# A decoder layer on one core: MLP weight sums by accumulating DMA with reordered products, and half of the last gate in seven products

## The chip, the core and the metric

The kernel runs on one core of a Trainium2 chip. Its engines each work through their own instruction list in order and meet by semaphores: PE (TensorE, matmuls), DVE (VectorE, elementwise), ACT (ScalarE, activations and copies), POOL (GpSimd, here an issuer of DMAs) and SP (SyncE, the issuer of the other DMAs). The metric is device time in microseconds of one execution; the median of three runs stands for a kernel.

## The reference, cut to what matters

One layer, 256 rows (`SEQ`) of 2048 columns (`D_MODEL`), all float32, `D_FF` = 8192:

```python
x = x + merged @ w_out[i]                       # two attention mixers, gated: not touched here
hm = rmsnorm(x, g_mlp[i])
x = x + jnp.square(jax.nn.relu(hm @ w_up[i])) @ w_down[i]
hp = rmsnorm(x, g_ple[i])
x = x + (p[i] @ w_ple_proj[i]) * jax.nn.sigmoid(hp @ w_ple_gate[i])
```

The change touches the product with `w_down` and the last line's product with `w_ple_gate` (2048 x 2048, "the gate").

## The kernel before

**Precision and splits.** Every weight comes as 1 MB of float32 in a `raw` tile (`load`, an SP DMA) and is split into a high part `wh` by ACT (L82) and a low part `wl` by DVE (L83), in two pieces of 128x1024; a tile pool gives `raw`, `wh` and `wl` three slots each, so a split can't begin before the slot of three pieces earlier has been read by PE. A product is three matmuls (high x high, high x low, low x high). Activations are split in the same way; where they are scaled, as at the turns, by L85 (ACT) and L86 (DVE).

**MLP.** The hidden dimension goes in eight groups s. `up_units(s)` computes hidden columns in 16 units of 8 pairs of matmuls (L525 of 512 columns, L526 of 256); `hidden` squares, and for the fast products forms four sums of the activations in `hr`, which has one buffer (L507 to L510), and splits them into a tile `u` of the pool `hid`. The down product of a group has two column halves. The second is plain (`plain_units`, 8 units of 12 matmuls, L627 to L629; results are added to the residual `xr` by `add_rows`, L454). The first (`fast_units`) uses a seven-product scheme on 2x2 blocks (as Strassen's): row blocks are the two 128-row tiles, the inner dimension and the columns are halved. Its seven products of 12 matmuls (L545, L547, L549) take four 1 MB quarters of the weight as they are, or sums of them: DVE adds one quarter to another in place (L559, four per group), `later(2, ...)`, two modelled microseconds after the product that still reads the old content. Partial results are copied from PSUM by ACT (`keep`, L555) and added to `xr` by DVE (L559 on `xr`, and L454).

**Order.** `together` interleaves the units of group s + 1's up product with group s's fast and plain units by fixed fractions; this makes seven periods between 713 and 1336 us. `advance` moves a modelled clock, and `later` emits work once that clock has come to its due time. What stands in an engine's list is fixed at build time.

**Gate.** After the last plain units (mixed with the embedding product, `embedding_units`) the residual is squared and summed (`squares_rows`) and turned: `turn` transposes with PE (L465, 8 per call) and splits. Four column groups of 96 matmuls follow (L724 to L726), two PSUM banks each, 16 loads of 1 MB. `gate_out` takes each result: ACT sigmoid (L712), DVE times the embedding (L713) and plus the residual (L714), DMA out.

Of the kernel before, what the change touches and what calls it, by code (L numbers as in the profile page):

```python
# [9 lines left out]
F32 = mybir.dt.float32  # L10
# [6 lines left out]
P = 128  # L17
# [42 lines left out]
def layer_kernel(ctx: ExitStack, tc: tile.TileContext, xt, xm, pt, gains, qkg, cst,  # L60
# [433 lines left out]
    FAST = [(s, 0) for s in range(7)]  # L494

    def hidden(s, fast):
# [40 lines left out]
    def fast_units(s, n, f):  # L537
# [46 lines left out]
        pz = bank("at")  # L584
        product(pz, S1, b[0, 0], True)
        z0 = keep(pz, 0)
        sum_later(b[0, 0], b[1, 1])
        yield
        sums()
        product(px, S2, b[0, 0], False)  # L590
        s2 = keep(px, 1)
        sum_later(b[0, 0], b[1, 0])
        yield
        sums()
        pw = bank("at")
        product(pw, A22, b[0, 0], True)
        w0 = keep(pw, 0)
        sum_later(b[0, 1], b[1, 1])
        yield
        py = bank("at")  # L600
        product(py, A12, b[1, 0], True)
        add(xr[1][:, left[0]], s1)
        add_rows(1, c1, py, r2[:, 1:2])
        yield
        sums()
        product(px, S3, b[0, 1], False)
        add(xr[0][:, left[0]], w0)
        add_rows(0, c1, px, r2[:, 0:1])
        add(xr[0][:, left[1]], z0)
        add_rows(0, c2, px, r2n)  # L610
        yield
        product(pz, S4, b[1, 1], False)
        nc.vector.tensor_tensor(xr[1][:, left[1]], xr[1][:, left[1]], s2, op=ALU.subtract)
        add_rows(1, c2, pz, r2[:, 1:2])
        yield

    def plain_units(s, n, u):

        for j in range(2):
# [15 lines left out]
            for tt in range(2):  # L635
                add_rows(tt, (2 * n + j) * PIECE, ps[tt], r2[:, tt:tt + 1])
# [16 lines left out]
    def embedding_units():  # L653
        em.extend(mw.tile([P, D], F32, tag="quart", name=f"em{tt}", bufs=4) for tt in range(2))
# [62 lines left out]
    for g in range(4):  # L717
# [10 lines left out]
        for tt in range(2):  # L728
            gate_out(g, tt, ps[tt], 0, PIECE)
# [64 lines left out]
```

## Time and profile before

| | us |
|---|---|
| median of three runs | 1487.3 (1486.57 to 1488.2) |
| the profiled execution | 1486.83 |
| its span | 1485.1 |
| PE busy | 1470.0 (99%) |
| DVE, ACT busy | 1002.1 (67%), 839.2 (57%) |
| seven MLP periods | 713 to 1336, 89.0 each |
| last MLP products and embedding | 1336 to 1390 |
| gate | 1390 to 1479, then results out until 1485.1 |

PE is the engine that sets the time. Matmuls overlap in it, so a start is a better mark than a busy time: from the start of one to the start of the next is what a matmul costs. In brackets behind an instruction of the timeline stands how long its engine was idle before it, and which instruction released it. The granted clock of PE is 1.00 at 2.4 GHz and 0.50 at 1.2 GHz.

### The profile page before, as it was taken

What the parts mean: (1) busy time and instruction counts of PE and PEld (TensorE: products, weight loads), DVE (VectorE), ACT (ScalarE), POOL (GpSimd) and SP (SyncE); (2) the same over time, 40 slices, a digit from 0 to 9 for tenths busy, and PEclk for the clock granted to TensorE, in tenths of its full rate; (3) what the DMA queues carried; (4) which work ended last, traced back from release to release, by engine and by line L of the source; (5) the groups of instructions that cost most, each with busy time, mean ns of one, the idle gap of its engine ahead of it and who ended that gap; (6) DMA issues with size and microseconds to landing.
All of it is one profiled execution on the core that took longest, in us unless ns stands there. A gap on an engine that the chain in (4) does not pass through costs nothing.

```text
span 1485.1 us, 17838 instructions
## 1 busy us (share of the span) xinstructions
PE 1470.0 (99%) x6960; PEld 1209.4 (81%) x6960; DVE 1002.1 (67%) x1209; ACT 839.2 (57%) x1084; POOL 49.2 (3%) x65
## 2 busy tenths in 40 slices
PE   8999999999999999999999999999999999999998
PEld 6788888888888888888787887878888788888886
DVE  5975555455555555556878879788787878766654
ACT  6545555488834444546655655656565655656543
POOL 0641000000000000000000000000000000000000
PEclk9999999999999999999999999999999999999999
DMA  8555544544455555557455564645546465444563
GB/s 334 197 193 179 172 167 169 174 167 171 171 197 197 173 197 184 185 193 289 142 201 195 175 225 141 227 168 197 200 157 238 144 205 194 154 144 167 206 218 109
DMA packets 40341, 279.09 MB, mean 188 GB/s; under 512 B 4624, under 2 KB 4880, under 8 KB 7104
## 3 DMA queue, kind: packets, MB, share of 16 engines
q1 hardware_dynamic: 39600, 275.01, 53.4%
q0 software_dynamic: 512, 2.92, 0.5%
q8 instruction: 54, 0.88, 0.2%
q14 instruction: 31, 0.25, 0.0%
q10 hardware_dynamic: 144, 0.02, 0.0%
HBM read 275.83 MB, written 2.10 MB: 187 GB/s over the span
## 4 chain that ended last, share of the span: by engine, by line
PE 91%; DVE 4%; issue 2%; ACT 1%; DMA 1%; SPq 0%; DVEq 0%; ACTq 0%
PE ps_mm L525 15%; PE ps_mm L139 13%; PE ps_mm L138 13%; PE ps_mm L137 13%; PE ps_mm L526 8%; PE ps_mm L628 4%; PE ps_mm L629 4%; PE ps_mm L627 3%; PE ps_at L547 3%; PE ps_at L545 2%; PE ps_at L549 2%; DVE wl L83 2%; ACT wh L82 1%; PE ps_at L725 1%; PE ps_at L724 1%
## 5 line engine op out<-in xcount | busy, mean ns | idle before, releaser
L83 DVE TENSOR_TENSOR wl<-raw,wh 128x1024 fp32r<-128x1024 f32 (+1 forms) x462 | 563.9, 1229 | 336.4 <-ACT wh L82 330.6
L82 ACT ACTIVATE wh<-raw 128x1024 fp32r<-128x1024 f32 (+1 forms) x462 | 484.9, 1053 | 388.6 <-PE ps_mm L139 209.4
L525 PE MATMUL ps_mm<-h,wh 128*128 128x512 f32 x1024 | 366.0, 398 | 0.0
L526 PE MATMUL ps_mm<-h,wl 128*128 128x256 f32 x1024 | 287.2, 281 | 0.4
L137 PE MATMUL ps_mm<-wh,h 128*128 128x512 f32 x640 | 254.9, 399 | 2.0 <-ACT wh L82 1.7
L138 PE MATMUL ps_mm<-wl,h 128*128 128x512 f32 x640 | 250.9, 392 | 1.2 <-DVE wl L83 1.1
L139 PE MATMUL ps_mm<-wh,h 128*128 128x512 f32 x640 | 250.8, 392 | 0.0
L525 PEld LDWEIGHTS ps_mm<-h,wh 128*128 128x128 f32 x1024 | 192.3, 188 | 46.2 <-ACT wh L82 2.2
L526 PEld LDWEIGHTS ps_mm<-h,wl 128*128 128x128 f32 x1024 | 193.2, 189 | 8.1 <-DVE wl L83 3.1
L83 DVE TENSOR_TENSOR wl<-quart,wh 128x1024 fp32r<-128x1024 f32 x98 | 120.0, 1224 | 83.7 <-ACT wh L82 83.5
L82 ACT ACTIVATE wh<-quart 128x1024 fp32r<-128x1024 f32 x98 | 104.0, 1061 | 123.4 <-PE ps_mm L525 89.1
L138 PEld LDWEIGHTS ps_mm<-wl,h 128*128 128x128 f32 x640 | 120.9, 189 | 27.9 <-DVE wl L83 3.9
L137 PEld LDWEIGHTS ps_mm<-wh,h 128*128 128x128 f32 x640 | 120.6, 189 | 28.1 <-ACT wh L82 4.4
L139 PEld LDWEIGHTS ps_mm<-wh,h 128*128 128x128 f32 x640 | 120.7, 189 | 25.5
L628 PE MATMUL ps_mm<-wl,u 128*128 128x512 f32 x256 | 101.9, 398 | 4.0 <-DVE wl L83 3.9
L629 PE MATMUL ps_mm<-wh,u 128*128 128x512 f32 x256 | 100.2, 391 | 0.0
L627 PE MATMUL ps_mm<-wh,u 128*128 128x512 f32 x256 | 98.0, 392 | 0.0
L547 PE MATMUL ps_at<-wl,u 128*128 128x512 f32 x196 | 80.4, 410 | 0.0
L545 PE MATMUL ps_at<-wh,u 128*128 128x512 f32 x196 | 78.6, 401 | 0.0
L549 PE MATMUL ps_at<-wh,u 128*128 128x512 f32 x196 | 76.8, 392 | 0.0
L559 DVE TENSOR_TENSOR quart<-quart 128x2048 f32<-128x2048 f32 x28 | 64.0, 2287 | 0.5
L628 PEld LDWEIGHTS ps_mm<-wl,u 128*128 128x128 f32 x256 | 48.1, 188 | 18.3 <-DVE wl L83 9.3
(198 smaller groups left out, 1704.8 us busy)
## 6 DMA issues: line engine op xcount, KB each, us to landing
raw<-in_wa SPq DMA_DIRECT2D x79, 1024.0 KB, 4.8
raw<-in_wup SPq DMA_DIRECT2D x64, 1024.0 KB, 4.8
raw<-in_wdn SPq DMA_DIRECT2D x36, 1024.0 KB, 4.8
quart<-in_wdn SPq DMA_DIRECT2D x28, 1024.0 KB, 4.8
raw<-in_wo SPq DMA_DIRECT2D x16, 1024.0 KB, 4.8
raw<-in_wpg SPq DMA_DIRECT2D x16, 1024.0 KB, 4.8
raw<-in_wba SPq DMA_DIRECT2D x8, 1024.0 KB, 4.8
raw<-in_wbb SPq DMA_DIRECT2D x8, 1024.0 KB, 4.7
```

Source lines behind the costliest of these rows:

```text
L82: nc.scalar.activation(hi, src, AF.Copy)
L83: nc.vector.tensor_tensor(lo, src, hi.bitcast(F32), op=ALU.subtract)
L137: nc.tensor.matmul(ps[tt], lhs[kt][:, 0, t], wh, start=kt == 0, stop=False)
L138: nc.tensor.matmul(ps[tt], lhs[kt][:, 0, t], wl, start=False, stop=False)
L139: nc.tensor.matmul(ps[tt], lhs[kt][:, 1, t], wh, start=False, stop=kt == last)
L525: nc.tensor.matmul(ps, wh, flat(h2[kt]), start=kt == 0, stop=False)
L526: nc.tensor.matmul(ps[:, :T], wl, h2[kt][:, 0, :], start=False, stop=kt == DT - 1)
L545: nc.tensor.matmul(ps, f[k][:, 0, a, :], wh, start=start and k == 0, stop=False, skip_group_check=not start)
L547: nc.tensor.matmul(ps, f[k][:, 0, a, :], wl, start=False, stop=False, skip_group_check=not start)
L627: nc.tensor.matmul(ps[tt], u[k][:, 0, a, :], wh, start=i + k == 0, stop=False)
L628: nc.tensor.matmul(ps[tt], u[k][:, 0, a, :], wl, start=False, stop=False)
L629: nc.tensor.matmul(ps[tt], u[k][:, 1, a, :], wh, start=False, stop=last)
```

## The change

**Weight sums in the MLP.** The four quarter tiles are gone. A tile `chain` (two buffers) is loaded with the first quarter; the running sums are made by DMAs that add in memory: `add_loaded` issues two of 512 KB from POOL after each product that read `chain`, three times per group. One other quarter is loaded into `right`, and DVE adds to it the quarter b11 (L569 of the changed kernel). b10 and b11 now come through the shared `raw` slots (14 loads there per period instead of 12; 19 MB per period from memory instead of 16). The seven products come in the order A11, A12, S1, S4, S2, S3, A22; partial results are not kept by ACT but added to `xr` at once from PSUM, by eight `add_rows` per group that are delayed by `later(0.6, ...)` or more into the next unit. The results of plain units are delayed in the same way.

**Gate.** Columns 0 to 1023 stay plain (`gate_plain`), columns 1024 to 2047 go by seven products over all rows (`gate_fast`), each of 24 matmuls (L792, L794, L795), mixed by `together`; 360 matmuls in all instead of 384. `turn_pair` turns two 128-column blocks at a time: four transposes (L686), two copies into `hr` (L690), four sums (L498 to L501), a split of 128x1024 on ACT and one on DVE. Two of the eight turned pairs (`h3u`) and the weights of the fast half (`gq`) live in the pool `hid`. Loads: 24 MB instead of 16 (`product` asks for its weight once per half, so A12's quarter is loaded twice), with 12 accumulating DMAs of 512 KB among them. `finish` adds a kept partial to the last one before `gate_out`.

```diff
-        px = bank("at")
-        product(px, A11, b[0, 0], True)
-        s1 = keep(px, 1)
-        sum_later(b[0, 0], b[0, 1])
-        yield
-        sums()
...
+        def add_loaded(q, i, j):
+            for k in range(0, 4, 2):
+                nc.gpsimd.dma_start(q[:, k:k + 2, :].rearrange("p k c -> p (k c)"),
+                                    wdn[s, n, i, j, :, k * PIECE:(k + 2) * PIECE],
+                                    accum_op=ALU.add)
...
+        chain = quarter("chain", 2, 0, 0)
         px = bank("at")
+        product(px, A11, chain, True)
+        add_loaded(chain, 0, 1)
+        later(0.6, add_rows, 1, c1, px, r2[:, 1:2])
+        yield
+        py = bank("at")
+        product(py, A12, load(wdn[s, n, 1, 0], 4, PIECE), True)
+        later(0.6, add_rows, 1, c1, py, r2[:, 1:2])
+        yield
+        pz = bank("at")
+        product(pz, S1, chain, True)
+        add_loaded(chain, 1, 1)
+        later(0.6, add_rows, 0, c2, pz, r2[:, 0:1])
+        right = quarter("right", 2, 0, 1)
+        yield
+        b11 = load(wdn[s, n, 1, 1], 4, PIECE)
+        product(pz, S4, b11, False)
+        later(0.6, add_rows, 1, c2, pz, r2[:, 1:2])
+        later(2, add, right, b11)
+        yield
+        product(px, S2, chain, False)
+        add_loaded(chain, 1, 0)
...
             for tt in range(2):
-                add_rows(tt, (2 * n + j) * PIECE, ps[tt], r2[:, tt:tt + 1])
+                args = tt, (2 * n + j) * PIECE, ps[tt], r2[:, tt:tt + 1]
+                if s < 7:
+                    later(0.6 + 1.5 * tt, add_rows, *args)
...
+    def turn_pair(k):
+        tp = bank("at")
+        for i in range(2):
+            for tt in range(2):
+                o = (2 * i + tt) * P
+                nc.tensor.transpose(tp[:, o:o + P],
+                                    xr[tt][:, (2 * k + i) * P:(2 * k + i + 1) * P], ident)
+        r = mw.tile([P, 8, P], F32, tag="hr", name="hr", bufs=1)
+        for i in range(2):
+            nc.scalar.activation(r[:, 2 * i:2 * i + 2, :].rearrange("p a t -> p (a t)"),
+                                 tp[:, i * T:(i + 1) * T], AF.Copy,
+                                 scale=gn[:, 2, 2 * k + i:2 * k + i + 1])
+        four_sums(r)
+        u = pair_tile(k)
+        split(u[:, 0], u[:, 1], r)
...
     def finished(g):
-        later(3, turn, g, h3, 2)
+        later(3, turn_pair, 2 * g)
+        later(4.5, turn_pair, 2 * g + 1)
...
+        chain = quarter(0, 0, room)
+        px, py = bank("at"), bank("at")
+        yield from product(px, A11, lambda c: chain[c], True, (0, 1))
+        keep_later("x", px)
+        yield
+        yield from product(py, A12, lambda c: load(wpg[1, 1, 0, c], 4, PIECE), True)
+        finish_later(0.6, 1, 0, "x", py, ALU.add)
...
+    together((0.9, 16, gate_plain()), (1.9, 14, gate_fast()))
```

**Three places in the order.** Names carry the number of their tile, `L` the line in the kernel that the row is of. First DVE in an MLP period of before, where an up unit's `hr` sums and low parts surround sums of quarters (L559):

```order
L507 TENSOR_TENSOR hr_8380<-hr_8380 128x128
L508 TENSOR_TENSOR hr_8380<-hr_8380 128x128
L83 TENSOR_TENSOR wl_8451<-quart_8431,wh_8450 128x1024
L509 TENSOR_TENSOR hr_8380<-hr_8380 128x128
L559 TENSOR_TENSOR quart_8431<-quart_8431,quart_8433 128x2048
L510 TENSOR_TENSOR hr_8380<-hr_8380 128x128
L83 TENSOR_TENSOR wl_8487<-raw_8484,wh_8486 128x1024
L83 TENSOR_TENSOR wl_8491<-raw_8484,wh_8490 128x1024
L83 TENSOR_TENSOR u_8386<-hr_8380,u_8386 128x1024
L532 TENSOR_TENSOR hs_8403<-ps_mm_8404,ev_8479 128x256
L559 TENSOR_TENSOR quart_8433<-quart_8433,quart_8435 128x2048
L83 TENSOR_TENSOR wl_8510<-raw_8507,wh_8509 128x1024
```

The like place of the changed kernel, DVE's list after the third and fourth fast product (`L535 hs` belongs to an up unit, `L454` are result adds, `chain` and `right` the new weight tiles):

```order
L83 TENSOR_TENSOR wl_7202<-raw_7199,wh_7201 128x1024
L454 SCALAR_TENSOR_TENSOR xr0_247<-ps_at_7154,r2_5039,xr0_247 128x512
L83 TENSOR_TENSOR wl_7206<-raw_7199,wh_7205 128x1024
L569 TENSOR_TENSOR right_7177<-right_7177,raw_7289 128x2048
L535 TENSOR_TENSOR hs_7126<-ps_mm_7127,ev_7196 128x256
L83 TENSOR_TENSOR wl_7225<-raw_7222,wh_7224 128x1024
L83 TENSOR_TENSOR wl_7229<-raw_7222,wh_7228 128x1024
L83 TENSOR_TENSOR wl_7292<-raw_7289,wh_7291 128x1024
L454 SCALAR_TENSOR_TENSOR xr0_247<-ps_mm_7010,r2_5039,xr0_247 128x512
L83 TENSOR_TENSOR wl_7303<-raw_7289,wh_7302 128x1024
L535 TENSOR_TENSOR hs_7126<-ps_mm_7221,ev_7264 128x256
L454 SCALAR_TENSOR_TENSOR xr1_248<-ps_mm_7011,r2_5039,xr1_248 128x512
L83 TENSOR_TENSOR wl_7318<-raw_7315,wh_7317 128x1024
```

The L559 sums of quarters between the low parts are gone but for one (L569); L454 result adds now stand there.

Second, ACT at the start of the gate before (`h3_2`, `h3_3` are turned columns, `wh` gate weights):

```order
L82 ACTIVATE wh_11084<-raw_11078 128x1024
L85 ACTIVATE h3_2_10766<-ps_at_11036,gn_75 128x256
L85 ACTIVATE h3_2_10766<-ps_at_11045,gn_75 128x256
L85 ACTIVATE h3_2_10766<-ps_at_11036,gn_75 128x256
L85 ACTIVATE h3_2_10766<-ps_at_11045,gn_75 128x256
L82 ACTIVATE wh_11125<-raw_11123 128x1024
L85 ACTIVATE h3_3_10767<-ps_at_11054,gn_75 128x256
L85 ACTIVATE h3_3_10767<-ps_at_11063,gn_75 128x256
L85 ACTIVATE h3_3_10767<-ps_at_11054,gn_75 128x256
```

and of the changed kernel (`h3u` are the last two turned pairs, `wh_11093` the high part of the fast half's first weight):

```order
L232 ACTIVATE junk_11019,ss2_5047<-xr1_248 128x512
L214 ACTIVATE rs_11102<-rv_11100 128x2
L690 ACTIVATE hr_11056<-ps_at_11051,gn_75 128x256 x2
L82 ACTIVATE h3u_11063<-hr_11056 128x1024
L690 ACTIVATE hr_11077<-ps_at_11072,gn_75 128x256 x2
L82 ACTIVATE h3u_11084<-hr_11077 128x1024
L82 ACTIVATE wh_11093<-gq_11087 128x1024
L82 ACTIVATE wh_11114<-gq_11087 128x1024
```

The first fast weight's split has come to stand behind both turned pairs. Third, PE at the same place before:

```order
L724 MATMUL ps_at_11006<-wh_11080,h3_1_10765 128x512
L725 MATMUL ps_at_11006<-wl_11081,h3_1_10765 128x512
L465 MATMUL ps_at_11054<-idt_84,xr0_247 128x128
L465 MATMUL ps_at_11054<-idt_84,xr1_248 128x128
L465 MATMUL ps_at_11054<-idt_84,xr0_247 128x128
L465 MATMUL ps_at_11054<-idt_84,xr1_248 128x128
L465 MATMUL ps_at_11063<-idt_84,xr0_247 128x128
L465 MATMUL ps_at_11063<-idt_84,xr1_248 128x128
L465 MATMUL ps_at_11063<-idt_84,xr0_247 128x128
L465 MATMUL ps_at_11063<-idt_84,xr1_248 128x128
```

and of the changed kernel:

```order
L748 MATMUL ps_mm_11022<-wh_11029,h3_3_10838 128x512
L750 MATMUL ps_mm_11022<-wl_11030,h3_3_10838 128x512
L751 MATMUL ps_mm_11022<-wh_11029,h3_3_10838 128x512
L686 MATMUL ps_at_11072<-idt_84,xr0_247 128x128
L686 MATMUL ps_at_11072<-idt_84,xr1_248 128x128
L686 MATMUL ps_at_11072<-idt_84,xr0_247 128x128
L686 MATMUL ps_at_11072<-idt_84,xr1_248 128x128
L792 MATMUL ps_at_11091<-wh_11093,h3_0_10689 128x512
L794 MATMUL ps_at_11091<-wl_11094,h3_0_10689 128x512
L795 MATMUL ps_at_11091<-wh_11093,h3_0_10689 128x512
```

The transposes of the last pair are followed directly by the fast half's first product (L792, which reads the high part; L794 reads the low part `wl_11094`).

## Rows read from the trace of the kernel before

**Rows 1.** The page, table of engines: busy time, share, instructions

```profile
PE 1470.0 (99%) x6960; PEld 1209.4 (81%) x6960; DVE 1002.1 (67%) x1209; ACT 839.2 (57%) x1084; POOL 49.2 (3%) x65
```

**Rows 2.** Windows, an MLP period and the gate: busy by engine, clock, DMA share, GB/s

```profile
802.00:891.00 89.00, 88.49 (x438) 72.25 (x437) 72.39 (x83) 52.32 (x63) 0.00 (x0) 1.00 0.55 189
1390.00:1479.00 89.00, 89.00 (x401) 73.34 (x399) 49.61 (x59) 42.15 (x51) 0.00 (x0) 1.00 0.50 172
```

**Rows 3.** Timeline, PE, up pairs: start, us, what; idle before in brackets

```profile
821.63 0.39 PE L525 MATMUL ps_mm<-h,wh 128*128 128x512 f32 x1
...
825.86 0.40 PE L525 MATMUL ps_mm<-h,wh 128*128 128x512 f32 x1
```

**Rows 4.** Timeline, PE: the gate's first matmul, eight transposes, its last matmul

```profile
1389.88 0.39 PE L724 MATMUL ps_at<-wh,h 128*128 128x512 f32 x1
...
1393.97 1.04 PE L465 MATMUL ps_at<-idt,xr 128*128 128x128 f32 x8
...
1478.64 0.39 PE L726 MATMUL ps_mm<-wh,h 128*128 128x512 f32 x1
```

**Rows 5.** Timeline, DVE and PE, about a sum of quarters

```profile
805.22 2.28 DVE L559 TENSOR_TENSOR quart<-quart 128x2048 f32<-128x2048 f32 x1
...
807.63 1.22 DVE L83 TENSOR_TENSOR wl<-raw,wh 128x1024 fp32r<-128x1024 f32 x1
808.90 0.50 PE L628 MATMUL ps_mm<-wl,u 128*128 128x512 f32 x1 [0.44 <-DVE wl L83]
```

**Rows 6.** Waits, 713 to 1336: total us, times, longest

```profile
PE ps_mm L628 <- DVE wl L83: 3.9, 7, 1.2
```

**Rows 7.** Timeline, ACT, a keep

```profile
812.12 0.69 ACT L555 ACTIVATE cp<-ps_at,r 128x512 f32<-128x512 f32 x1 [1.94 <-PE ps_at L549]
```

**Rows 8.** Groups by form, 713 to 1336: count, busy us, mean ns, idle before

```profile
L83 DVE TENSOR_TENSOR wl<-raw,wh 128x1024 fp32r<-128x1024 f32 x169 | 203.9, 1220 | 35.5 <-ACT wh L82 33.5
L82 ACT ACTIVATE wh<-raw 128x1024 fp32r<-128x1024 f32 x169 | 178.0, 1057 | 106.6 <-PE ps_mm L525 56.5 <-PE ps_at L549 34.9 <-PE ps_mm L629 15.1
L559 DVE TENSOR_TENSOR quart<-quart 128x2048 f32<-128x2048 f32 x28 | 64.0, 2287 | 0.5
L454 DVE SCALAR_TENSOR_TENSOR xr<-ps_at,r,xr 128x512 f32<-128x512 f32 x21 | 15.7, 748 | 2.7 <-PE ps_at L549 2.7
L507 DVE TENSOR_TENSOR hr<-hr 128x128 f32<-128x128 f32 x25 | 7.1, 283 | 0.0
```

**Rows 9.** Timeline, DVE and PE, result adds of a plain unit

```profile
844.27 1.40 DVE L454 SCALAR_TENSOR_TENSOR xr<-ps_mm,r,xr 128x512 f32<-128x512 f32 x2
845.59 2.35 DVE L83 TENSOR_TENSOR wl<-raw,wh 128x1024 fp32r<-128x1024 f32 x2
...
846.40 0.39 PE L525 MATMUL ps_mm<-h,wh 128*128 128x512 f32 x1
846.86 0.39 PE L526 MATMUL ps_mm<-h,wl 128*128 128x256 f32 x1
```

**Rows 10.** DMA issues of the span: engine, count, KB each, us to landing

```profile
raw<-in_wdn SPq DMA_DIRECT2D x36, 1024.0 KB, 4.8
...
xr<-in_xm POOLq DMA_DIRECT2D x2, 1024.0 KB, 9.7
```

**Rows 11.** Groups by form, 1390 to 1486

```profile
L713 DVE TENSOR_TENSOR o<-o,em 128x512 f32<-128x512 f32 x8 | 5.4, 692 | 7.5 <-ACT o L712 7.5
...
L85 ACT ACTIVATE h<-ps_at,gn 128x256 fp32r<-128x256 f32 x8 | 3.6, 473 | 1.6 <-DVE h L86 0.9 <-PE ps_at L465 0.7
```

**Rows 12.** The kernel's start: PE's timeline, then windows

```profile
9.80 0.73 PE L137 MATMUL ps_mm<-wh,h 128*128 128x512 f32 x2 [1.73 <-ACT wh L82]
...
10.00:12.00 2.00, 2.00 (x6) 1.28 (x6) 1.57 (x4) 1.71 (x4) 0.00 (x0) 0.68 1.09 440
12.00:14.00 2.00, 2.00 (x7) 1.52 (x6) 2.00 (x5) 1.74 (x5) 0.00 (x0) 0.50 0.97 403
```

**Rows 13.** Timeline, DVE, the last adds

```profile
1480.39 1.28 DVE L714 TENSOR_TENSOR o<-o,xr 128x512 f32<-128x512 f32 x2
```

More of the change, by code (lines that the diff above doesn't have):

```diff
@@ L494, in layer_kernel, with four_sums @@
     FAST = [(s, 0) for s in range(7)]
+    def four_sums(r):
+        a21, a11, a22, a12 = (r[:, i, :] for i in range(4))
+        nc.vector.tensor_tensor(r[:, 4, :], a11, a21, op=ALU.subtract)
+        nc.vector.tensor_tensor(r[:, 5, :], a21, a22, op=ALU.subtract)
+        nc.vector.tensor_tensor(r[:, 6, :], r[:, 5, :], a11, op=ALU.subtract)
+        nc.vector.tensor_tensor(r[:, 7, :], r[:, 6, :], a12, op=ALU.add)
     def hidden(s, fast):
@@ new lines, in fast_units @@
+        add_loaded(chain, 1, 1)
+        later(0.6, add_rows, 0, c2, pz, r2[:, 0:1])
+        right = quarter("right", 2, 0, 1)
+        yield
+        b11 = load(wdn[s, n, 1, 1], 4, PIECE)
[5 more added lines that the diff above has]
+        add_loaded(chain, 1, 0)
+        later(0.6, add_rows, 1, c2, px, r2n[:, 1:2])
+        yield
+        product(px, S3, right, False)
@@ L615, in fast_units @@
+        later(0.6, add_rows, 0, c1, px, r2[:, 0:1])
+        later(2.1, add_rows, 0, c2, px, r2n[:, 0:1])
+        yield
+        pw = bank("at")
+        product(pw, A22, chain, True)
+        later(0.6, add_rows, 0, c1, pw, r2[:, 0:1])
         yield
@@ L653, in embedding_units @@
     def embedding_units():
-        em.extend(mw.tile([P, D], F32, tag="quart", name=f"em{tt}", bufs=4) for tt in range(2))
+        em.extend(mw.tile([P, D], F32, tag="right", name=f"em{tt}", bufs=2) for tt in range(2))
         praw = mw.tile([P, 2, T], F32, tag="hs", name="praw", bufs=2)
@@ L677, in layer_kernel, with pair_tile @@
     h3 = []
+    def pair_tile(k):
+        if k < 4:
+            return block([P, 2, 8, P], F32R, f"h3_{k}", blk)
+        if k < 6:
+            return mw.tile([P, 2, 8, P], F32R, tag="chain", name="h3q", bufs=2)
+        return hid.tile([P, 2, 8, P], F32R, tag="hid", name="h3u")
+    def turn_pair(k):
[10 more added lines that the diff above has]
+                                 scale=gn[:, 2, 2 * k + i:2 * k + i + 1])
+        four_sums(r)
+        u = pair_tile(k)
+        split(u[:, 0], u[:, 1], r)
+        h3.append(u)
     def finished(g):
-        if g == 0:
-            h3.extend(new_acts("h3_", pool=blk))
         for tt in range(2):
             squares_rows(tt, g, ss2, mw.tile([P, PIECE], F32, tag="cp", name="junk", bufs=5))
-        later(3, turn, g, h3, 2)
+        later(3, turn_pair, 2 * g)
+        later(4.5, turn_pair, 2 * g + 1)
     def last_units(u):
         for n in range(2):
-            yield from plain_units(7, n, u)
-            finished(2 * n)
-            finished(2 * n + 1)
+            units = plain_units(7, n, u)
+            for i in range(8):
+                next(units)
+                if i % 4 == 3:
+                    finished(2 * n + i // 4)
+                yield
     hids = [[]]
@@ L751, in quarters, with halves @@
     return np.ascontiguousarray(w).reshape(k // 1024, n // 1024, 2, 2, P, 4 * 512)
+def halves(w):
+    k, n = w.shape
+    w = w.reshape(k // 1024, 4, 2, P, n // 1024, 2, 512).transpose(4, 2, 5, 0, 3, 1, 6)
+    return np.ascontiguousarray(w).reshape(n // 1024, 2, 2, k // 1024, P, 4 * 512)
 def columns(a):
```

178 lines of the change are left out of this document (111 added, 67 removed).

## The prediction

> **What bounds the kernel now.** I read the page's table of engines first: TensorE (PE) is busy for 99% of the span [rows 1], so an edit pays only by taking matmuls away or stalls out of PE's stream, and costs what it puts in front of PE. The span is 1485.1 us, the profiled run 1486.83, so 1.73 lie outside it; the median of the runs is 1487.3, 0.47 above that run. A measurement here tells about 0.2%, 3 us, from no change: "same" means 1484.3 to 1490.3.
>
> Then I looked stage by stage. One MLP period of 89.0 us shows PE busy for 88.49 [rows 2], but a late operand partly hides in the modelled ends of matmuls, so I take starts instead. Twelve up pairs from 821.63 to 825.86 give 0.3525 us a pair [rows 3]. The gate's 384 matmuls of 512 columns and 16 transposes begin at 1389.88 and the last matmul starts at 1478.64 [rows 4]; with 0.131 us a transpose (8 in 1.04 us [rows 4]) a matmul is (88.76 + 0.23 - 2.1) / 384 = 0.2263 us. A period holds 128 pairs and 84 + 96 = 180 matmuls of 512 columns: 45.1 + 40.7 = 85.8 us of pure stream in 89.0. So **at most 3.2 us a period, 22 us in seven, are stalls**, and no edit to the other engines can give back more there. The gate has no stall to give: 89.00 busy of 89.00, DVE (VectorE) 49.61 [rows 2].
>
> Next, who ends these stalls. A sum of quarters on VectorE starts at 805.22 and holds it 2.28 us; the next low part starts at 807.63, and PE's L628 begins at 808.90 [rows 5]. PE's two L627 before it were due to end by about 808.3, so 0.6 us are lost. The list of waits has this one 7 times, 3.9 us in all [rows 6]: once a period. A second loss is the keep on ACT (ScalarE): at 812.12 it had stood 1.94 us waiting for PE, with a weight split queued behind [rows 7]. By the same comparison of starts through the period, sums and keeps cost about 1.5 us a period; some 1.1 more come where a fast unit's splits follow an up unit's with three weight slots, which the change leaves; the rest is spread thin.
>
> **MLP: removed.** Per period four sums of 2.29 us leave VectorE as such [rows 8]; one comes back (`right` + b11), so 6.9 us of VectorE go, and four keeps of 0.69 us leave ACT [rows 7]. VectorE and ACT bound nothing on average, so this counts only through the 1.5 us a period: at most 10.5 us.
>
> **MLP: added and moved.** The eight result adds become `add_rows` of 0.75 us [rows 8], each 0.6 us or more after its product, in the middle of the next unit's splits. The order shows two of them and a hidden sum (0.74 + 0.42 + 0.74) between the low parts before `wl_7318`. The like of it is in the trace: two adds of 1.40 us at 844.27 push a low part to 845.59 and L526 to 846.86, 0.46 instead of 0.23 after its L525 [rows 9]. Priced so, this place loses 0.7 us against its due time, the sum at L569 0.3, the first split of the reduced chain 0.3, together 1.3. Where the next split's slot is not yet free, the wait is one that was there before; I take half as new, **0.65 a period**. Net 1.5 - 0.65 = 0.85 a period, **-6 us over seven**; bounds 0 (new waits equal the old) and -16 (1.5 and most of the 1.1 go, nothing new).
>
> The six accumulating DMAs of 512 KB a period are in no row. Between two uses of `chain` the order leaves 17 to 22 us for two of them. From below, a plain 1 MB load lands in 4.8 us; from above, a GpSimd-issued 1 MB load in the crowded start took 9.7 [rows 10], twice that for reading and rewriting is 19.4. I take 10 and so no stall; the upper bound is a rival. SP's loads get shorter windows in places, 9 to 14 us, still above 4.8.
>
> A rule speaks against this. Two DMAs issued by GpSimd stand beside a VectorE that is busy 72 of 89 us [rows 2]. The Trainium skill, "SBUF — State Buffer", section "SBUF: two separate sides", says that such a DMA's descriptors are written by GpSimd's own cores, and that a VectorE operation holding the shared port pair keeps them from it; "Who interferes with whom" there adds that `tensor_tensor` has no two-port mode but contends with GpSimd's reads when both inputs lie in SBUF, as the splits' do. No row here shows it; if it held each pair up until a gap in VectorE, the sum would go to rival C. By its fit in "DMA: Bandwidth & Descriptors", section "Anatomy of one DMA — SWDGE (gpsimd) path", 512 KB would take an estimated 3.2 us and the term would stay zero.
>
> **Gate: removed.** Seven products of 24 matmuls and the plain half's 192 make 360 for 384: 24 x 0.2263 = **-5.4 us**, surely on the path.
>
> **Gate: the last turns.** This is the largest term. Before, after the last MLP matmul the first two gate weights are split, and the turned columns (0.473 us each [rows 11]) come between weights that are far ahead of PE. After, PE's order is 12 products, 6, four transposes, 6, four transposes, and then at once L792, the first fast product; ACT's is two copies to `hr`, split to h3u, two copies, split, and only then `wh_11093`. `hr` has one buffer, so the second pair waits for the first's low part. From the gate's start G: PE has work until 24 x 0.2263 + 1.04 = G + 6.5. The chain: first transposes end at G + 4.65; two copies 0.95 (L85's row [rows 11] is the nearest), to 5.6; four sums 0.8 (0.28 each, overlapping [rows 8]), to 6.4; ACT split 1.05, to 7.5; low part 1.22, to 8.8 with hand-overs; two copies to 9.8; sums to 10.55; ACT split to 11.65; `wh_11093` to 12.7; `wl_11094` to 14.1 (split rows from [rows 8]). L792 alone may go at 12.7, L794 needs the low part: **PE stands 14.1 - 6.5 - 0.2 = 7.4 us**; what is queued behind on PE is the whole gate, and no cover exists, since the plain matmuls come after in its order. Bounds 6.5 (hand-overs of nothing) and 8.
>
> After such a pause the clock: PE waited 1.73 us before 9.80 at the kernel's start, and the granted clock then was 0.68 and 0.50 in the two slices from 10 to 14 [rows 12], the lower level of 1.2 GHz for about 3.3 us; lost (0.32 + 0.50) x 2 = **+1.6 us** (0 if the clock stays up, 2 if it is longer).
>
> **Gate: smaller terms, all up.** Loads: 24 MB come instead of 16, A12's halves twice. Those for S3 have 4.6 to 4.8 us in the order from free buffer to use, against 4.8 to land [rows 10], beside accumulating DMAs: **+1.5** (0 to 4, from one load twice as long). Turning the earlier six pairs beside the embedding adds four sums and whole-tile splits each, about 2 us of VectorE a pair, in a stage without slack measured at PE: **+0.75** (0 to 2). Four `gate_out` operations, 2 x 0.69 + 2 x 0.69 = 2.8 us [rows 11], stand before a low part at the plain half's first end: **+1.0** (0.5 to 2). The tail: one `finish` of about 0.68 ahead of the sigmoid, and a single chain: last add ends about 3.5 us after PE against 2.6 now (1480.39 + 1.28, less the last matmul's end, 1478.64 + 0.39 [rows 4, 13]): **+0.9** (0.5 to 1.3).
>
> **Sum**: -6 - 5.4 + 7.4 + 1.6 + 1.5 + 0.75 + 1.0 + 0.9 = +1.75. On the profiled run 1488.6, on the median 1489.05: I say 1489.
>
> **Rivals.** A: the MLP's stalls go nearly whole. For it: their releasers are the removed sums and what queues behind them; against it: the delayed adds and slot waits. -16 for -6 gives 1479. D: the pause at the gate is not there (the copies or splits come earlier than my walk, or the fast product's first part is ready). For: the order is fixed but the walk's times are mine; against: four operations on ACT and one `hr` stand before it. Without 9.0: 1480. B, slower: the gate's loads come late beside the accumulating DMAs: three of its parts with windows under 7.5 us each late by 1.6 to 3.5 us, where the sum had 1.5 in all: +5 to +10, 1494 to 1499. It decides from a landing above about 6 us there; the start's loads show that crowding can do this (9.7 [rows 10]). C: two accumulating DMAs take over 17 us, so every second fast product stands: three pairs a period by 1 to 5 us, seven periods: +20 to +100. That the sums don't leave VectorE is no case; the order shows them gone.
>
> **How the numbers follow.** Forecast 0.44 (1484 to 1494; of it faster 0.04, same 0.24, slower 0.16), A 0.20 (1476 to 1483), D 0.10 (1478 to 1482), B 0.18, C 0.08. Faster 0.04 + 0.20 + 0.10 = 0.34, same 0.24, slower 0.16 + 0.18 + 0.08 = 0.42. The range leaves out C, B's top third and a little below A: 1477 to 1498. The forecast's own range is 1484 to 1494.
>
> **What would show it.** An MLP period of 88.1 to 88.3 instead of 89.0, with L628 no longer waiting; A gives 86.7. A PE wait of 7 us about 6.5 us into the gate, released by VectorE's low part of a gq tile, and a granted clock near 0.5 behind it; D shows none. B: PE waits in the gate ended by DMA. C: waits of fast products ended by the accumulating DMAs. Wrong in the whole would be a gain over 10 us with the pause present: then the stalls of the MLP were mis-sized.

## The result and the profile after

| | before | after |
|---|---|---|
| median, us | 1486.93 (4 runs) | 1498.01 (1497.35 to 1498.84, 4 runs) |
| ratio to before, 95% interval | | 1.0078 (1.0063 to 1.0093) |
| span of the profiled execution | 1485.1 | 1496.6 |

The changed kernel is slower by 11.1 us, where 1489 was forecast as likeliest and 1498 was the end of the range. PE's share of the span fell from 99% [rows 1] to 98%. The page's table of engines of the changed kernel:

```profile
PE 1467.5 (98%) x6936; PEld 1203.7 (80%) x6936; DVE 991.6 (66%) x1230; ACT 845.2 (56%) x1080; POOL 96.0 (6%) x119
```

The windows of an MLP period (from one group's first fast matmul to the next one's) and of the gate (first to last matmul); columns as in [rows 2]:

```profile
802.70:891.05 88.35, 87.89 (x439) 72.08 (x437) 66.44 (x80) 50.06 (x58) 5.19 (x6) 1.00 0.75 226
1386.45:1490.20 103.75, 91.04 (x369) 70.21 (x367) 72.92 (x81) 56.90 (x65) 10.38 (x12) 0.93 0.78 226
```

The two answer [rows 2]: the period came down from 89.0 to 88.35, with VectorE 6 us less busy; the gate went from 89 us with PE never idle to 103.75 with PE busy for 91 of it, its granted clock at 0.93 on average. So the time went into the gate, and the MLP gave some back. From starts of PE's matmuls:

| stretch, us | before | after | difference |
|---|---|---|---|
| start of the span to the MLP's first up matmul (not touched) | 664.84 | 665.19 | +0.35 |
| from there to the gate's first matmul | 725.04 | 721.26 | -3.8 |
| gate, first matmul to start of the last | 88.76 | 103.53 | +14.8 |
| start of the last matmul to the end of the span | 6.42 | 6.65 | +0.23 |

The first line differs by up to 3 us between profiled executions (663.4 to 666.4 over all kernels here, the same instructions in each), so stretches are compared by their own length below.

What PE waits for in the gate of the changed kernel, from the list of waits (total us, times, longest; the two DMA lines are waits of ACT and DVE that PE's stand behind):

```profile
PE ps_at L792 <- ACT wh L82: 9.5, 2, 6.6
ACT wh L82 <- DMA raw<-in_wpg: 6.3, 2, 4.9
PE ps_at L794 <- DVE wl L83: 1.9, 3, 0.7
DVE gq L124 <- DMA raw<-in_wpg: 1.4, 1, 1.4
PE ps_mm L750 <- DVE wl L83: 0.9, 1, 0.9
```

Two long pauses of PE make up the first line. **The first** is at the gate's start. PE's timeline: the last pair's transposes, then the first fast product:

```profile
1392.36 0.60 PE L686 MATMUL ps_at<-idt,xr 128*128 128x128 f32 x4
1399.52 0.79 PE L792 MATMUL ps_at<-wh,h 128*128 128x512 f32 x1 [6.55 <-ACT wh L82]
1400.97 0.80 PE L794 MATMUL ps_at<-wl,h 128*128 128x512 f32 x1 [0.66 <-DVE wl L83]
```

and ACT's list beside it, where each instruction waits for the one before it in the chain:

```profile
1391.23 0.84 ACT L690 ACTIVATE hr<-ps_at,gn 128x256 f32<-128x256 f32 x2 [1.14 <-PE ps_at L686]
1393.14 1.06 ACT L82 ACTIVATE h3u<-hr 128x1024 fp32r<-128x1024 f32 x1 [1.07 <-DVE hr L501]
1395.55 0.84 ACT L690 ACTIVATE hr<-ps_at,gn 128x256 f32<-128x256 f32 x2 [1.35 <-DVE h3u L83]
1397.46 1.06 ACT L82 ACTIVATE h3u<-hr 128x1024 fp32r<-128x1024 f32 x1 [1.07 <-DVE hr L501]
1398.43 1.99 ACT L82 ACTIVATE wh<-gq 128x1024 fp32r<-128x1024 f32 x2
```

This is the walk of the prediction, step for step: copies, sums, split, low part, copies (held by the one `hr` buffer), sums, split, and only then the weight. The clock behind it (windows as before; PEclk is the third number from the end):

```profile
1394.00:1398.00 4.00, 0.00 (x0) 0.00 (x0) 2.40 (x5) 1.57 (x4) 0.00 (x0) 0.95 1.01 424
1398.00:1402.00 4.00, 1.83 (x4) 1.14 (x5) 3.45 (x4) 3.36 (x4) 0.56 (x1) 0.50 0.59 250
1402.00:1406.00 4.00, 4.00 (x14) 3.23 (x13) 2.41 (x3) 1.67 (x2) 1.17 (x2) 0.70 0.85 140
```

Counted from start to start, against 0.2275 us a matmul and 0.11 a transpose, PE lost 6.7 and 1.2 us at the two waits and 1.7 in matmuls at the lower level until 1404.5: 9.6 us.

**The second pause** is 23 us later and has another cause. POOL, SP, ACT and PE in their timelines:

```profile
1408.00 0.86 POOL L781 DMA_DIRECT2D gq<-in_wpg  x1 [4.79 <-DVE wl L83]
1410.75 0.86 POOL L781 DMA_DIRECT2D gq<-in_wpg  x1 [1.88 <-DVE wl L83]
1411.88 0.33 SPq L91 DMA_DIRECT2D raw<-in_wpg  x1
1421.14 1.06 ACT L82 ACTIVATE wh<-raw 128x1024 fp32r<-128x1024 f32 x1 [4.92 <-DMA raw<-in_wpg]
1422.25 0.80 PE L792 MATMUL ps_at<-wh,h3q 128*128 128x512 f32 x1 [2.98 <-ACT wh L82]
```

SP issues the load of A12's second half at 1411.88, when its `raw` slot comes free; it lands 9.15 us later in the chain that ended last, where plain loads took 4.8 [rows 10], and two accumulating DMAs were issued just before it. The issues of the gate (KB each, median us to landing) show that all its transfers are slow:

```profile
raw<-in_wpg SPq DMA_DIRECT2D x11, 1024.0 KB, 7.0
gq<-in_wpg POOLq DMA_DIRECT2D x12, 512.0 KB, 7.1
gq<-in_wpg SPq DMA_DIRECT2D x4, 1024.0 KB, 11.3
```

and the windows show what came of the pause:

```profile
1418.00:1422.00 4.00, 1.27 (x6) 0.70 (x4) 0.00 (x0) 0.86 (x1) 0.00 (x0) 0.94 1.01 377
1422.00:1424.00 2.00, 1.29 (x2) 0.78 (x3) 1.23 (x1) 0.60 (x2) 0.00 (x0) 0.50 1.07 451
1424.00:1428.00 4.00, 4.00 (x11) 3.03 (x11) 2.09 (x2) 1.71 (x2) 0.00 (x0) 0.50 0.95 356
```

From start to start, 3.1 us are lost at L792, 1.0 at the L794 behind it and 2.3 in the slow matmuls until 1428.3: 6.5 us (6.3 in the expectations). Two smaller places follow. ACT loads the table of the sigmoid between two weight splits (1431.46, 1.28 us), and PE loses 1.8 us from 1433 to 1436.5; DVE has a sum of quarters and four result operations ahead of low parts, and PE loses 1.5 us from 1447.1 to 1451.6:

```profile
1431.46 1.28 ACT L733 ACT_TABLE_LOAD   x1
1433.39 1.99 ACT L82 ACTIVATE wh<-raw 128x1024 fp32r<-128x1024 f32 x2
...
1444.22 2.29 DVE L124 TENSOR_TENSOR gq<-gq,raw 128x2048 f32<-128x2048 f32 x1 [1.41 <-DMA raw<-in_wpg]
...
1447.56 1.29 DVE L734 TENSOR_TENSOR o<-o,em 128x512 f32<-128x512 f32 x2
1448.76 1.29 DVE L735 TENSOR_TENSOR o<-o,xr 128x512 f32<-128x512 f32 x2
1449.97 2.35 DVE L83 TENSOR_TENSOR wl<-raw,wh 128x1024 fp32r<-128x1024 f32 x2
1451.24 0.50 PE L794 MATMUL ps_at<-wl,h 128*128 128x512 f32 x1 [0.75 <-DVE wl L83]
```

Sum for the gate: 9.6 + 6.5 + 1.8 + 1.5 = 19.4 at these four places, and 1.7 in lags of 0.2 us and less. Against it stand 5.4 for the 24 matmuls and 0.9 for eight transposes that now come ahead of the gate (16 were in it before, 8 are now). That gives the 14.8.

### The profile page after: what moved, and what is told of

It reads as the page before. It is cut to its first block, busy times and chain, and to the rows that moved or that the text cites. A ratio compares the mean times of both kernels' runs of the same rounds, so it can differ in the third digit from the quotient of the medians.

```text
span 1496.6 us, 17942 instructions
## 1 busy us (share of the span) xinstructions
PE 1467.5 (98%) x6936; PEld 1203.7 (80%) x6936; DVE 991.6 (66%) x1230; ACT 845.2 (56%) x1080; POOL 96.0 (6%) x119
## 4 chain that ended last, share of the span: by engine, by line
PE 91%; DVE 4%; DMA 2%; ACT 1%; issue 1%; SPq 0%; ACTq 0%; DVEq 0%
PE ps_mm L528 16%; PE ps_mm L139 13%; PE ps_mm L137 13%; PE ps_mm L138 13%; PE ps_mm L529 8%; PE ps_mm L616 4%; PE ps_mm L618 4%; PE ps_mm L617 4%; PE ps_at L550 3%; PE ps_at L548 3%; PE ps_at L552 3%; DVE wl L83 2%; DMA raw<-in_wpg 1%; PE ps_at L794 1%; DMA raw<-in_wa 1%
## 5 line engine op out<-in xcount | busy, mean ns | idle before, releaser
L83 DVE TENSOR_TENSOR wl<-raw,wh 128x1024 fp32r<-128x1024 f32 (+1 forms) x482 | 588.9, 1229 | 365.7 <-ACT wh L82 359.5
L82 ACT ACTIVATE wh<-raw 128x1024 fp32r<-128x1024 f32 (+1 forms) x482 | 506.5, 1054 | 445.0 <-PE ps_mm L139 209.2
L564 POOL DMA_DIRECT2D chain<-in_wdn x42 | 36.4, 866 | 1142.2 <-DVE hs L535 593.8
L617 PE MATMUL ps_mm<-wl,u 128*128 128x512 f32 x256 | 100.2, 391 | 0.0
L83 DVE TENSOR_TENSOR wl<-chain,wh 128x1024 fp32r<-128x1024 f32 x56 | 68.4, 1224 | 29.2 <-ACT wh L82 28.5
L82 ACT ACTIVATE wh<-chain 128x1024 fp32r<-128x1024 f32 x56 | 59.3, 1059 | 48.3 <-PE ps_mm L528 22.7
L616 PEld LDWEIGHTS ps_mm<-wh,u 128*128 128x128 f32 x256 | 48.1, 188 | 10.3 <-DVE hs L535 0.3
```

Of the source, the lines that this page charges most:

```text
L82: nc.scalar.activation(hi, src, AF.Copy)
L83: nc.vector.tensor_tensor(lo, src, hi.bitcast(F32), op=ALU.subtract)
L616: nc.tensor.matmul(ps[tt], u[k][:, 0, a, :], wh, start=i + k == 0, stop=False)
L617: nc.tensor.matmul(ps[tt], u[k][:, 0, a, :], wl, start=False, stop=False)
```

## The experiments

The theory after the result: the MLP part gains what was forecast, and the gate loses it by two separate pauses, one from the chain of the last turns on ACT and DVE, one from loads that the accumulating DMAs make late; the clock falls behind each. Rivals: the accumulating DMAs cost in the MLP too; the gate lacks DMA time as a whole, whatever is loaded when; the pauses are VectorE's and ScalarE's amount of work and only move. "Up to gate" below is from the first up matmul to the gate's first, "gate" from its first matmul to the start of its last, both in the profiled execution.

| kernel | median, us | ratio to before (95%) | up to gate | gate |
|---|---|---|---|---|
| after | 1498.01 | 1.0078 (1.0063 to 1.0093) | 721.26 | 103.53 |
| e1_mlp_only | 1480.67 | 0.9962 (0.9947 to 0.9977) | 719.92 | 88.78 |
| e2_gate_only | 1503.0 | 1.0109 (1.0094 to 1.0125) | 726.41 | 103.63 |
| e3_a12_once | 1495.49 | 1.0063 (1.0046 to 1.008) | 721.61 | 100.70 |
| e4_turn_staged | 1486.16 | 0.9999 (0.999 to 1.0008) | 721.07 | 91.22 |
| e5_gate_no_accum | 1491.63 | 1.0039 (1.0026 to 1.0052) | 722.40 | 96.53 |
| e6_table_early | 1497.97 | 1.008 (1.0063 to 1.0096) | 721.56 | 103.25 |
| e7_mlp_no_accum | 1497.77 | 1.0083 (1.0067 to 1.0098) | 721.73 | 103.48 |
| e8_three_mends | 1486.32 | 1.0006 (0.9997 to 1.0016) | 722.03 | 90.83 |
| e10_gate_dve_sums | 1487.57 | 1.0007 (0.9997 to 1.0017) | 721.60 | 93.53 |
| e11_staged_no_accum | 1483.11 | 0.9972 (0.9962 to 0.9982) | 721.99 | 87.68 |
| e12_adds_at_once | 1481.38 | 0.9962 (0.9949 to 0.9976) | 720.66 | 88.76 |
| e13_mlp_only_again | 1482.26 | 0.9969 (0.9958 to 0.9981) | 721.30 | 88.76 |

**e1_mlp_only: the MLP part alone.** The turns and the gate are those of before.

```diff
-    together((0.9, 16, gate_plain()), (1.9, 14, gate_fast()))
+    for g in range(4):
+        ps = [bank("mm") if g % 2 else bank("at") for _ in range(2)]
...
+            gate_out(g, tt, ps[tt], 0, PIECE)
```

> Only the MLP part of the change; turns and gate as before. Theory (the MLP part gains what its periods show, 0.33 in the first and about 0.7 in each of the next six; the loss is all in the gate): 1482, between 1481 and 1483.5. Rival (the accumulating DMAs or the delayed adds cost as much as the sums saved, and the gain seen belongs to the run): 1486 or more.

Faster by 6.1 us, a little beyond the theory's end; the stretch up to the gate is 5.1 shorter (3.7 in e13, the same kernel) and the rest lies ahead of the MLP. The waits in the seven periods show the wait of [rows 6] gone and a smaller one in its place:

```profile
PE ps_mm L529 <- DVE wl L83: 2.3, 5, 0.5
```

**e2_gate_only: the gate part alone**, with the MLP of before (its two free `quart` tiles stand in for `chain`).

```diff
...
-        later(3, turn, g, h3, 2)
+        later(3, turn_pair, 2 * g)
+        later(4.5, turn_pair, 2 * g + 1)
...
```

> Only the gate part (pair turns, seven products in the second half); the MLP as before. Theory (two parts that add up): 1486.9 + 11.1 + 4.5 = 1502.5, between 1501 and 1504. Rival (the gate suffers from what the new MLP leaves behind, its late adds or DMAs): under 1499.

1503.0: the parts add up, -6 and +16. The gate takes what it took in the changed kernel, so nothing that the new MLP leaves behind slows it; and the stretch up to it is 1.4 longer than before, which is the price of the pair turns beside the embedding: from the last up matmul to the gate's first it takes 58.6 us in the kernel before, e1, e12 and e13, and 60.0 in e2 and the changed kernel.

**e5_gate_no_accum: no accumulating DMAs in the gate.**

```diff
-                if then:
-                    add_loaded(b(c), c, *then)
```

> The changed kernel without the twelve accumulating DMAs of the gate: its chain quarters stay unsummed, so this leaves out part of the computation. Theory (A12's second load, 9.15 us from issue to landing, shares the DMA engines with two accumulating DMAs): it lands in about 5 us, the 6.3 us about 1422 go, 1491.7, between 1490 and 1493.5. Rival (the SP loads alone crowd each other, or the slot is what comes late): landing stays above 7 us, 1495 or more.

1491.63, the gate 7.0 us shorter: the pause about 1422 and the low clock behind it are gone, and the first pause stands unchanged at 6.55. The gate's plain loads land in 4.9 instead of 7.0 us at the median:

```profile
raw<-in_wpg SPq DMA_DIRECT2D x11, 1024.0 KB, 4.9
gq<-in_wpg SPq DMA_DIRECT2D x4, 1024.0 KB, 11.1
```

So the load was late because of what ran beside it, not because its slot came free late. The second line is a warning: four plain loads, issued within 2 us at the gate's start, take 11.1 us at the median without any accumulating DMA in the gate.

**e4_turn_staged: the last two turns taken apart.** Transposes first, copies and sums later, the split later still, with a second `hr` buffer (two `cp` buffers less make room), so that the first fast weight is split ahead of them.

```diff
...
-        later(3, turn_pair, 2 * g)
-        later(4.5, turn_pair, 2 * g + 1)
+        if g == 3:
+            later(2, turn_pair, 6, 1, 3)
+            later(2.1, turn_pair, 7, 4.2, 1.3)
+        else:
+            later(3, turn_pair, 2 * g)
+            later(4.5, turn_pair, 2 * g + 1)
...
```

> The changed kernel, with the last two pair turns taken apart: transposes after the first gate unit, copies and sums and the split later, two hr buffers, so that the first fast weight's split stands ahead of them in ScalarE's and VectorE's lists. Theory (the 6.9 + 1.2 us pause at the gate's start and the low clock behind it, 9.6 in all, are the chain of two turns on ScalarE and VectorE): 2 to 3 are left, 1491, between 1489.5 and 1493. Rival (the pause is VectorE's and ScalarE's amount of work there, and only moves): 1495 or more.

1486.16, 12 us faster than the changed kernel, well beyond the theory. Of the first pause only this is left in the timeline:

```profile
1395.84 0.50 PE L768 MATMUL ps_mm<-wl,h 128*128 128x512 f32 x1 [0.53 <-DVE wl L83]
```

where 0.8 us are lost, so nearly all of the 9.6 went, and the low clock with it. But e4 takes away a second thing as well. Its last turned pairs come later, so the pool `hid` has room for the first fast weight early, and its load is issued 57 us ahead of where the changed kernel issues it, in a row of four (first the changed kernel, then e4):

```profile
1386.66 2.02 SPq L770 DMA_DIRECT2D gq<-in_wpg  x4
1329.19 0.90 SPq L788 DMA_DIRECT2D gq<-in_wpg  x2
```

In the changed kernel the first of the four landed at 1395.1. With a split and a low part behind it (1.06 and 1.22 us) L794 could have started at about 1397.5, an estimate, against 1400.97 measured and 1393 due. So the chain of turns set the length of the pause, but more than half of it would have stood for this load; e4 doesn't separate the two.

The load after it, A12's, is late as before:

```profile
ACT wh L82 <- DMA raw<-in_wpg: 9.9, 3, 6.4
PE ps_at L810 <- ACT wh L82: 2.6, 1, 2.6
```

but costs 4.3 us instead of 6.5, and the table load no longer costs PE anything.

**e3_a12_once: A12's halves loaded once.**

```diff
-        yield from product(py, A12, lambda c: load(wpg[1, 1, 0, c], 4, PIECE), True)
+        a12 = {}
+        yield from product(py, A12, lambda c: a12[c] if c in a12 else
+                           a12.setdefault(c, load(wpg[1, 1, 0, c], 4, PIECE)), True)
```

> The changed kernel, but each half of A12's quarter in the gate is loaded once instead of twice (two 1 MB loads less). Theory (the pause of 3.1 us near 1422 and the low clock behind it come from the second half's load, issued at 1411.88 only when a slot came free, and landed 9.15 us later): 6.3 us go, 1491.5, between 1490 and 1493.5. Rival (the gate is short of DMA time as a whole, and the next load is late instead): no more than 2 us go, 1496 or more.

Between the two: the gate is 2.8 us shorter, not 6.3 or more. The pause at A12 is gone, but the next load is late instead. VectorE, in its timeline, waits for b11 with the sum for `right`, and the low parts stand behind the sum:

```profile
1426.95 2.29 DVE L124 TENSOR_TENSOR gq<-gq,raw 128x2048 f32<-128x2048 f32 x1 [1.37 <-DMA raw<-in_wpg]
1429.16 0.69 DVE L735 TENSOR_TENSOR o<-o,xr 128x512 f32<-128x512 f32 x1
1429.76 2.36 DVE L83 TENSOR_TENSOR wl<-raw,wh 128x1024 fp32r<-128x1024 f32 x2
```

PE loses 1.2 us there at a split that stands behind the table load in ScalarE's list, 3.1 at the low parts, and 2.9 more at the lower clock. The rival holds in part: 2 MB less do not relieve the stretch.

**e6_table_early: the sigmoid's table loaded at the gate's start.**

```diff
-    later(6, lambda: rms.append(rows_norm(ss2, "rt2", mw)))
+    def gate_norm():
+        rms.append(rows_norm(ss2, "rt2", mw))
+        nc.scalar.activation(r2n, rms[1], AF.Sigmoid)
...
```

> The changed kernel with one small sigmoid on ScalarE right after the gate's norm, so that the table of the sigmoid (1.28 us) is loaded while ScalarE waits at the gate's start. Theory (the 1.7 us lost about 1434 to 1436 are the table load ahead of a weight split): 1496.3, between 1495.3 and 1497.2. Rival (the load then lengthens the chain of the turns at the gate's start by as much): 1497.7 or more.

No gain, and the rival is nearer. The 1.8 us at 1434 are gone, but the first pause grew from 6.7 to 7.0 with slow matmuls until 1405.3, 0.8 later than in the changed kernel, and from 1446 to 1452 PE loses 1.9 us where it lost 1.5. The table load is no term that can be taken out of the sum by itself.

**e8_three_mends: e4, e3 and e6 at once.**

> The changed kernel with three mends at once: last turns in stages (as e4_turn_staged), A12's halves loaded once (as e3_a12_once), the sigmoid's table early (as e6_table_early). Theory (three separate losses): e4's 1486.2 less 2.5 and 1.7, 1482, between 1480.5 and 1484. Rival (one loss hides behind another, and the accumulating DMAs keep the loads late): 1485 or more.

The rival: no better than e4 alone. The late load is b11's now. The chain of work that ended last:

```profile
1420.90 10.68 DMA raw<-in_wpg
```

and the waits of the gate:

```profile
DVE gq L124 <- DMA raw<-in_wpg: 4.9, 1, 4.9
PE ps_mm L772 <- DVE wl L83: 4.3, 2, 3.6
```

One load is on its way for 10.7 us. The load that PE comes to wait for is each time one under way beside accumulating DMAs: A12's second half in the changed kernel and e4, b11's in e3 and here.

**e11_staged_no_accum: e4 and e3, without the gate's accumulating DMAs.**

```diff
-                if then:
-                    add_loaded(b(c), c, *then)
```

> As e4_turn_staged with A12's halves loaded once, without the gate's accumulating DMAs: its chain quarters stay unsummed, so this leaves out part of the computation. It tells what the gate would take if both causes were gone. Theory (the turns and the late loads are the gate's two losses, and little else is): the gate from first to last matmul 84 to 86.5 us, 1480.5, between 1479 and 1482.5. Rival (the lists of VectorE and ScalarE alone keep PE waiting): gate over 88, 1484 or more.

The gate falls to 87.68, between the two expectations: with both causes away it is 1.1 us under that of before, although it holds 5.4 us less of matmuls. Of the rest of its loss 1.2 us are at a ScalarE split behind the table load, 1.6 at a low part behind a sum of quarters and the first result, and 0.8 at the last turns.

**e10_gate_dve_sums: the gate's chain sums by VectorE.** Plain loads into `raw` slots and adds of 2.29 us in place of the accumulating DMAs, with the edits of e4 and e3.

```diff
-            for k in range(0, 4, 2):
-                nc.gpsimd.dma_start(q[:, k:k + 2, :].rearrange("p k c -> p (k c)"),
...
+            raw = load(wpg[1, i, j, c], 4, PIECE)
+            nc.vector.tensor_tensor(q, q, raw, op=ALU.add)
```

> As e4_turn_staged with A12's halves loaded once, and the gate's chain sums made as the MLP's were before: each quarter half by a plain 1 MB load into a raw slot, added by VectorE in 2.29 us, six times; no accumulating DMA in the gate. Theory (in the gate the accumulating DMAs, not VectorE, are what is short): the waits for late loads go, the six sums put about 2 us back, 1482, between 1480 and 1484. Rival (22 MB through three raw slots and 14 us of sums on VectorE make as many pauses as the accumulating DMAs did): 1486 or more.

The rival: 1487.57, the gate 93.53. It has the more pauses, four of 1.0 to 2.1 us, with only one wait for a DMA behind them (2.5 us of ACT's). So the accumulating DMAs are not worse in the gate than sums on VectorE. Against e11, which leaves these sums out, the gate is 5.9 us longer with them on VectorE and 3.2 longer with them as accumulating DMAs (e8, which has e6's edit as well).

**e7_mlp_no_accum: no accumulating DMAs in the MLP.**

```diff
-        add_loaded(chain, 0, 1)
...
-        add_loaded(chain, 1, 1)
...
-        add_loaded(chain, 1, 0)
```

> The changed kernel without the 42 accumulating DMAs of the MLP: the chain quarters stay unsummed there, so this leaves out part of the computation. Theory (they are hidden: each pair has 17 us and more between uses and a DMA takes 6 us): no change, 1498, between 1496.5 and 1499.5. Rival (held up by VectorE or crowding the loads, they cost part of the MLP's gain): 1495 or less.

No change, 1497.77, with the stretch up to the gate at 721.73 against 721.26: in the MLP they are hidden. There, in the changed kernel, they land in 6.0 us at the median and leave the plain loads at 4.8:

```profile
raw<-in_wdn SPq DMA_DIRECT2D x43, 1024.0 KB, 4.8
chain<-in_wdn POOLq DMA_DIRECT2D x42, 512.0 KB, 6.0
```

**e12_adds_at_once and e13_mlp_only_again.** e13 is e1 once more; e12 is e1 with the result adds written right behind their products.

```diff
-        later(0.6, add_rows, 1, c1, px, r2[:, 1:2])
+        add_rows(1, c1, px, r2[:, 1:2])
...
```

> As e1_mlp_only (MLP part alone), but with the result adds written right behind their products instead of 0.6 us or more later. By the order the two adds of a plain unit then stand together ahead of an up unit's sum and two low parts, instead of one before and one after. Theory (the delayed adds are the 0.65 us a period that the change puts back, and standing together they hold up a low part more): slower than e1_mlp_only by 0.3 to 0.7 a period, 1483 to 1485.5. Rival (the delay itself is what costs): 1479 or less.

> e1_mlp_only once more, beside e12_adds_at_once on the same chip, in more rounds: 1480.7 again, between 1479.7 and 1482.5, so faster than the kernel before by 0.3 to 0.5%. If the first look was a lucky chip, 1484 or more.

e13: 1482.26, so e1's gain is 5 to 6 us. e12: 1481.38, neither theory; the delay is worth nothing that these runs can tell. Its waits in the periods fit that: 2.7 us in six places at a fast product's low part instead of 2.3 in five at an up pair's.

```profile
PE ps_at L550 <- DVE wl L83: 2.7, 6, 0.5
```

## Why the prediction was wrong, step by step

- **MLP, -6 (0 to -16): right.** Alone it gave 4.9 and 6.1 us in two sets of runs. From the first fast matmul to the last up matmul it takes 618.1 us before, 612.9 in the changed kernel and e1, and 613.6 in e13. L628 (L617 in the changed kernel) waits no more, the period is 88.2 to 88.35 after a first one of 89.1 (88.1 to 88.3 was written), and a new wait is where it was placed, at a low part behind a result add:

```profile
844.30 0.74 DVE L454 SCALAR_TENSOR_TENSOR xr<-ps_mm,r,xr 128x512 f32<-128x512 f32 x1
846.23 0.39 PE L529 MATMUL ps_mm<-h,wl 128*128 128x256 f32 x1 [0.46 <-DVE wl L83]
```

Rival A is out. That the delay of the adds causes the new wait is refuted by e12. No run took the adds themselves away, so their part in it is argued, not shown.
- **Accumulating DMAs in the MLP, 0: right** (e7). Rival C is out, at 6.0 us a DMA against the 17 between uses. The estimate by the fit in the Trainium skill, "DMA: Bandwidth & Descriptors", section "Anatomy of one DMA — SWDGE (gpsimd) path", was 3.2 us. The rows say 6.0 for an accumulating one, so the measurement decides.
- **24 matmuls, -5.4: right**, as far as it can be read: the gate's losses less 5.4, and less 0.9 for the eight transposes that the sum did not count, give its length.
- **The last turns, +7.4 and +1.6 for the clock: right.** 7.9 and 1.7 were lost, by the chain that the walk followed, and e4 took nearly all of it away. What the walk left out changed nothing here: the first fast weight landed so late that a shorter chain would have met a wait for it. Rival D is out.
- **The gate's loads, +1.5 (0 to 4): wrong, and this is the step that failed.** It cost 6.5. The text also named the wrong product: S3's quarter was loaded by 1402.4, long before its use, and the load that came late is A12's second half, issued 7.2 us before PE was due for it. The bound "one load twice as long" was right for the landing (9.15 against 4.8) and for the wait that it makes (3.1 and 1.0 at PE). What it left out is that such a pause brings the clock down again, 2.3 us more; the clock was priced for the first pause only. And the value was put near the lower bound without a row for it, since the only GpSimd-issued 1 MB load in the trace, 9.7 us [rows 10], stood at the other end. Rival B named this mechanism, its stage and its price (+5 to +10, from a landing above 6 us); it had a chance of 0.18 and was the case, though by one late load with the clock behind it and not by three.
- **Embedding and pair turns, +0.75: small miss**, 1.4, of which 0.9 is the eight transposes that came over from the gate. **`gate_out` before low parts, +1.0**: 1.5, with a late sum of quarters in it. **Tail, +0.9**: 0.23; the last add ends 3.6 us after the last matmul's start instead of 3.0, but one output DMA follows it instead of two, and the span ends sooner behind it.
- **Not in the sum: the table load** ahead of a split, 1.8 us in this order. In the gate of before the same load fell where PE did not wait. e6 shows that it is not additive. The lags of 0.2 us and less, 1.7 in all, were not in it either.

Adding what was measured, -3.8 up to the gate, +14.8 in it, +0.23 behind it and +0.35 ahead of the MLP, gives the 11.6 between the two spans. The mis-sized terms are 6.5 for 1.5, 1.8 and 1.7 for 0, and parts of 1 us.

What stays open is why a plain load beside two accumulating DMAs takes twice as long in the gate and 4.8 us in the MLP. Two tables point to an answer. In the MLP (713 to 1336) the packets of the accumulating DMAs (q0) took twice the time of plain ones (q1) for each MB; columns are packets, MB and their time as a share of 16 engines' span:

```profile
q1 hardware_dynamic: 15790, 114.15, 52.4%
q0 software_dynamic: 6048, 22.02, 20.3%
```

That is 0.92% a MB against 0.46%, and 5.3% against 2.5% in the gate (33.1% for 6.29 MB, 43.5% for 17.07). And loads stand more closely in the gate, four SP loads and four accumulating DMAs in the 17 us from 1401 on. The windows about the second pause, first the changed kernel's and then that of e5 (DMA share and GB/s at the end):

```profile
1406.00:1428.00 22.00, 18.56 (x70) 14.06 (x69) 10.67 (x9) 9.42 (x10) 1.73 (x2) 0.85 0.98 310
1406.00:1428.00 22.00, 22.00 (x95) 17.46 (x94) 12.89 (x12) 12.89 (x13) 0.00 (x0) 0.99 0.76 278
```

An MLP period had 0.75. This fits DMA engines that are full in the gate's stretch because each added MB took two MB's time, but no run varied the distance of the loads alone, so it is not shown.

The best kernel measured that computes the whole layer is the MLP part by itself, 1480.7 and 1482.3 us (1481.4 with the adds at once), 0.3 to 0.4% faster than the kernel before.

## What to carry to other kernels

Sums by accumulating DMA were hidden here in a long stage, where there is slack around them. Seven products in place of eight gained next to nothing in the short last stage, where turns, loads and sums come due at once: even with both causes away and the sums left out (e11), the gate won 1.1 us of the 6.3 that its matmuls and transposes had become shorter. Price the sums' DMAs by what else the DMA engines carry in that stretch, not by their landing time elsewhere. Where PE paused for 3 us and more here, another 1.5 to 2.9 us went in matmuls at the lower clock behind it, so such a wait is to be priced with that. When one late load is mended, look for the next in line before counting the gain.

## What the runs showed of the hardware that was not expected

- A plain 1 MB load next to accumulating DMAs landed in 9.15 to 10.7 us, and in 4.9 at the median in the same gate without them (e5). Four plain loads issued within 2 us took 11.1 there as well.
- An accumulating DMA's packets took about twice the time of plain ones for each MB, in the MLP (0.92% of the span of 16 engines against 0.46%) and in the gate (5.3% against 2.5%).
- An accumulating DMA of 512 KB landed in 6.0 us (MLP) and 7.1 us (gate) at the median, and took GpSimd 0.86 us to issue; 42 of them beside a VectorE that was busy for 66 of 88 us cost PE nothing that the time could tell (e7). The Trainium skill, "SBUF — State Buffer", section "SBUF: two separate sides", warns that VectorE can keep GpSimd from writing descriptors while it runs an operation in a two-port mode. No effect showed in the time here, but VectorE's work was mostly `tensor_tensor`, which by the same page has no such mode, so this is no test of that rule.
- Pauses of 2.75 to 3.8 us (e3, e4, e8 and the changed kernel) were followed by 1.5 to 2.9 us lost in matmuls at the clock's lower level (granted clock 0.50), and those of 6.7 to 7.0 us at the gate's start (e5, e6 and the changed kernel) by 1.7 to 2.6: the longer pause did not cost more behind it. In e10 one of 1.9 us was followed by such a stretch and one of 2.1 us was not.
